# Gate and up products of a SwiGLU layer: one 512-column product for both parts of x, with part of the block sums made earlier

## The chip, the cores and the metric

The kernel runs on one core of a Trainium2 chip (trn2). The metric is the device time of one execution in microseconds. The core has five engines with a queue of instructions each: TensorE (PE in the profile, with its weight loads as PEld), VectorE (DVE), ScalarE (ACT), GpSimd (POOL) and SyncE (SP). An engine takes its instructions in the order in which the program issued them; between engines, semaphores order the work. Here SP only issues DMAs, and POOL mostly does.

## The reference, cut to what matters

An encoder layer on 512 tokens of width 2048: a dilated window attention and a gated linear attention side by side, an output projection, then a SwiGLU feed-forward, all in float32.

```python
h = rmsnorm(x, attn_norm_w[l]);  proj = h @ w_in[l]
...                                    # attention and linear attention
x = x + mixed                          # mixed = concat(...) @ w_out[l]
h = rmsnorm(x, ffn_norm_w[l])          # (512, 2048)
x = x + (jax.nn.silu(h @ w_gate[l]) * (h @ w_up[l])) @ w_down[l]   # FFN_HIDDEN = 5632
return rmsnorm(x, final_norm_w)
```

The change lies in `h @ w_gate` and `h @ w_up`, two products of (512 x 2048) by (2048 x 5632).

## The kernel before

**Precision.** TensorE is given float32 in a rounded form (fp32r). Each operand is split in a rounded part (hi, a cast on ScalarE) and the rounding remainder (lo = value - hi, a subtraction on VectorE), and each product is made three times: hi x hi, hi x lo, lo x hi.

**Gate/up** (class `Feed`, built on `Blocks`). The hidden dimension is cut into 22 stretches of 256 columns; each stretch has a gate unit and an up unit, so there are 44 units, gate and up in turn (the first units are interleaved a little). A unit has 4 pieces of four 128-row blocks of the weight each (512 KB). Weights and tokens are multiplied by a Strassen-Winograd scheme with seven products in place of eight: it needs four sums of weight blocks per piece (`sums`, L1089 to L1091, VectorE), and sums of x made once (`pair_operands`). `split` casts three raw blocks and four summed blocks of a piece (L1101, ScalarE, 768 and 1024 columns), then subtracts (L1106, VectorE). A piece has 2 k-pairs x 7 products x 3 = 42 matmuls of 256 columns (L1147 to L1149); a unit accumulates over its pieces in four PSUM banks (two of the seven results share a bank in three cases). At the end `evac` combines the seven results on VectorE (L1158, L1166) in steps, one step per later piece; a gate unit is multiplied by the token scale (L1184) and goes through Silu (L1185, ScalarE); an up unit is multiplied by that (L1188) and POOL writes the result to `gd` in DRAM (L1190).

**Order.** `run` walks over the pieces. For piece i it issues: loads as slots allow (at most three raw pieces held), the sums of piece i + 2, the split of piece i + 1, the matmuls of piece i, and one step of the `evac` of the unit that ended (`run_urgent`). So the subtraction of piece i + 1 has to be done when TensorE has finished piece i.

**Slots.** SBUF tiles come from two sets, 70 slots of 512 columns (`s2`, a in the profile) and 16 of 1024 (`s4`, b); PSUM is 8 banks (`ps`). A slot that is given back goes to the end of a queue and the one that has been free longest is taken, so with few free ones a slot is soon used again, and its new user waits until the old user's readers are done, a DMA among them.

**Before gate/up.** `jobs` 0 to 5 are the projections for the attention, 6 to 11 those for the linear attention, 12 to 15 (`n_out`) the output projection. `run_job` takes half pieces of weights (512 columns by 128 rows), twelve matmuls of 512 columns each (L285 to L287 and L293 to L295), splits three halves ahead (L196, L197) and, between two halves, lets the attention and linear-attention work (`side`) go on by its rate; so the last attention heads run beside job 6 and the linear attention beside jobs 7 to 12. The down projection follows gate/up; it has its own `Blocks` and isn't touched.

Of the kernel before, what the change touches and what calls it, by code (L numbers as in the profile page):

```python
# [23 lines left out]
P = 128  # L24
# [93 lines left out]
def layer(nc, tc, x, attn_norm_w, w_in, rel_table, gw_f, gb_f, gw_b, gb_b, gla_norm_w, w_out,  # L118
# [7 lines left out]
    with tc.manual_schedule(), \  # L126
# [25 lines left out]
        state = {"credit": 0.0, "set": None}  # L152
# [96 lines left out]
        class Job:  # L249
            drop = None  # L250

# [11 lines left out]
        def run_job(j):  # L263
# [6 lines left out]
            for i in range(j.n):  # L270
# [690 lines left out]
        def half_split(src, n=512):  # L961

            if n == 512:
                hi, lo = s2.get(F32R), s2.get(F32R)
                return (hi, lo), hi.t, lo.t, hi.f
            o = s2.get(F32R, [P, 2, 256])
            return (o,), o.t[:, 0], o.t[:, 1], o.f[:, 0]

        def pair_operands(q, fs_):
# [10 lines left out]
            todo = []  # L980
            slots = []
            for src, n in ((f1.t[:, a], 256), (f2.t, 512), (t13.t, 512), (t24.t, 512)):
                sl, hi, lo, hf = half_split(src, n)
                slots += sl
                todo.append((src, hi, lo, hf))
            for i in range(4):
                src, hi, lo, hf = todo[i]
                act.copy(hi, src)
                sub(lo, src, hf)
                put((f1, f2, t13, t24)[i])  # L990
                if i % 2:
                    yield
            (_, b1h, b1l, _), (_, f2h, f2l, _), (_, t13h, t13l, _), (_, t24h, t24l, _) = todo
            xs[q] = dict(slots=slots, B11=(b1h, b1l), B21=(f2h[:, a], f2l[:, a]), B22=(f2h[:, z], f2l[:, z]),
                         T1=(t13h[:, a], t13l[:, a]), T3=(t13h[:, z], t13l[:, z]),
                         T2=(t24h[:, a], t24l[:, a]), T4=(t24h[:, z], t24l[:, z]))
# [62 lines left out]
        class Blocks:  # L1059
# [9 lines left out]
            def load(self):  # L1069
                while self.n_load < self.n and len(self.raw) < 3 and s4.free:  # L1070
                    w, k, n_kt, col, n = self.source(*self.seq[self.n_load])
                    r = s4.get(F32, self.shape(4))
                    sp.dma_start(out=r.t.rearrange("p a b c -> p (a b c)").rearrange("p (k c) -> p k c", k=n_kt),
                                 in_=w[k * P:(k + n_kt) * P, col:col + n].rearrange("(k p) c -> p k c", p=P))
                    self.raw[self.n_load] = r
                    self.n_load += 1

# [34 lines left out]
        class Feed(Blocks):  # L1112
# [3 lines left out]

            def __init__(self):
# [4 lines left out]
                self.begin(seq, 2, P)  # L1122

# [3 lines left out]

            def products(self, i, banks):
                st_ = self.sets.pop(i)
                piece = self.seq[i][1]  # L1130
                first, last = piece == 0, piece == self.per - 1
                a, z = slice(0, 256), slice(256, 512)
                A, B, C, E = (b.t for b in banks)
                for p in range(2):
                    q = 2 * piece + p
                    (rh, rl), (sh, sl) = st_
                    R = lambda n: (rh.t[:, p, n], rl.t[:, p, n])
                    Z = lambda n: (sh.t[:, p, n], sl.t[:, p, n])
                    x_ = xs[q]
                    prods = [(A[:, a], R(0), x_["B11"], True), (A[:, z], R(2), x_["B21"], False),  # L1140
                             (B[:, a], Z(2), x_["T2"], True), (C[:, a], Z(1), x_["T1"], True),
                             (C[:, z], Z(0), x_["T3"], False), (E[:, a], Z(3), x_["B22"], True),
# [462 lines left out]
```

## Time and profile before

| what | value |
|---|---|
| median of 3 runs | 2231.96 us (2231.88 to 2232.73) |
| the profiled execution's own time | 2234.08 us |
| its span | 2232.3 us |
| granted TensorE clock | 0.999 |
| gate/up stage (first matmul at 869.1, last at 1762.4 us) | 893 us, 7,392 matmuls of 256 columns |
| DMA over the span | 307.78 MB, mean 138 GB/s |

Times in the profile are microseconds. A row of the timeline gives start, duration, engine, line, operation, output <- input, shape and count; what stands in square brackets is how long the engine was idle before it and who released it. Matmuls are pipelined, so a row's duration is longer than the distance to the next one's start; it is the distances that add up. The same holds in part for VectorE and ScalarE, whose operations overlap by up to 0.1 us.

### The profile page before, as it was taken

To read this page: it belongs to the slowest core of one execution; us is meant where nothing else is said; L and a number is where in the kernel's file an instruction comes from. 1 tells how busy PE (TensorE), PEld (TensorE's weight loads), DVE (VectorE), ACT (ScalarE), POOL (GpSimd) and SP (SyncE) were. 2 spreads that over 40 slices of the span, in tenths; PEclk is the share of its full clock that TensorE was granted. 3 is DMA by queue.
4 is the path that set the end of the run, shared out by engine and by line. 5 is a ranking of instruction groups with operands and counts; after the bars stand their busy time and mean duration, and the time that the engine had idled before them with its cause. 6 is when DMAs were issued, how large, how long until landed. Compare 5 with 4: busy or idle time off the path is not lost.

```text
span 2232.3 us, 37013 instructions
## 1 busy us (share of the span) xinstructions
PE 2207.0 (99%) x14814; PEld 2034.4 (91%) x14814; DVE 1635.4 (73%) x2717; ACT 1002.7 (45%) x1637; POOL 116.2 (5%) x173
## 2 busy tenths in 40 slices
PE   8999999999999999999999999999999999999998
PEld 6888888888888888999999999999999999999986
DVE  4366665745454436988888888888888788988877
ACT  5344454444454344444434343444334565555543
POOL 0000000000000100000000000000000110022220
PEclk9999999999999999999999999999999999999999
DMA  6525625232314332333333333333333774588992
GB/s 206 158 68 154 177 79 147 85 123 64 97 57 151 128 127 76 113 115 124 114 114 123 114 123 114 114 125 115 122 120 116 247 179 171 185 198 184 237 372 80
DMA packets 211804, 307.78 MB, mean 138 GB/s; under 512 B 15375, under 2 KB 131263, under 8 KB 211632
## 3 DMA queue, kind: packets, MB, share of 16 engines
q1 hardware_dynamic: 192480, 259.37, 36.1%
q0 software_dynamic: 18256, 44.99, 8.5%
q8 instruction: 116, 1.90, 0.3%
q10 hardware_dynamic: 896, 1.06, 0.1%
q14 instruction: 56, 0.46, 0.1%
HBM read 246.58 MB, written 46.20 MB: 131 GB/s over the span
## 4 chain that ended last, share of the span: by engine, by line
PE 94%; DVE 2%; DMA 2%; ACT 1%; issue 0%; SPq 0%; ACTq 0%; DVEq 0%
PE ps L1149 13%; PE ps L1148 13%; PE ps L1147 13%; PE ps L293 6%; PE ps L294 6%; PE ps L295 6%; PE ps L285 5%; PE ps L287 5%; PE ps L286 5%; PE ps L1376 5%; PE ps L1375 5%; PE ps L1374 5%; PE ps L514 1%; PE ps L841 1%; DMA a<-md 1%; DMA b<-gd 1%
## 5 line engine op out<-in xcount | busy, mean ns | idle before, releaser
L1149 PE MATMUL ps<-a,b 128*128 128x256 f32 x2464 | 697.7, 283 | 2.9 <-DVE b L1106 2.9
L1147 PE MATMUL ps<-a,b 128*128 128x256 f32 x2464 | 697.4, 283 | 0.0
L1148 PE MATMUL ps<-a,b 128*128 128x256 f32 x2464 | 697.3, 283 | 0.0
L1101 ACT CAST b<-b 128x768 fp32r<-128x768 f32 x480 | 445.8, 942 | 533.4 <-DVE b L1106 285.9
L1106 DVE TENSOR_TENSOR b<-b,b 128x768 fp32r<-128x768 f32 x480 | 510.3, 1089 | 132.8 <-PE ps L1148 61.8
L1149 PEld LDWEIGHTS ps<-a,b 128*128 128x128 f32 x2464 | 473.0, 192 | 3.8 <-DVE b L1106 3.8
L1148 PEld LDWEIGHTS ps<-a,b 128*128 128x128 f32 x2464 | 473.0, 192 | 0.0
L1147 PEld LDWEIGHTS ps<-a,b 128*128 128x128 f32 x2464 | 473.0, 192 | 0.0
L197 DVE TENSOR_TENSOR a<-b,a 128x512 fp32r<-128x512 f32 x292 | 195.0, 686 | 126.9 <-ACT a L196 125.7
L1376 PE MATMUL ps<-b,a 128*128 128x256 f32 x896 | 253.7, 283 | 2.7 <-DVE a L1339 2.7
L1375 PE MATMUL ps<-b,a 128*128 128x256 f32 x896 | 253.6, 283 | 0.0
L1374 PE MATMUL ps<-b,a 128*128 128x256 f32 x896 | 253.6, 283 | 0.0
L196 ACT CAST a<-b 128x512 fp32r<-128x512 f32 x292 | 171.1, 617 | 55.8 <-DMA b<-in_w_down_dram 20.9
L293 PE MATMUL ps<-a,a 128*128 128x512 f32 x464 | 183.5, 396 | 0.0
L294 PE MATMUL ps<-a,a 128*128 128x512 f32 x464 | 181.2, 391 | 2.3 <-DVE a L197 2.1
L295 PE MATMUL ps<-a,a 128*128 128x512 f32 x464 | 180.9, 390 | 0.0
L1376 PEld LDWEIGHTS ps<-b,a 128*128 128x128 f32 x896 | 172.0, 192 | 2.9 <-DVE a L1339 2.9
L1375 PEld LDWEIGHTS ps<-b,a 128*128 128x128 f32 x896 | 172.0, 192 | 0.0
L1374 PEld LDWEIGHTS ps<-b,a 128*128 128x128 f32 x896 | 172.0, 192 | 0.0
L1089 DVE TENSOR_TENSOR b<-b 128x512 f32<-128x512 f32 x240 | 164.2, 684 | 7.2 <-DMA b<-in_w_up_dram 4.3
L285 PE MATMUL ps<-a,a 128*128 128x512 f32 x416 | 168.1, 404 | 0.0
L286 PE MATMUL ps<-a,a 128*128 128x512 f32 x416 | 163.1, 392 | 0.0
(224 smaller groups left out, 3071.2 us busy)
## 6 DMA issues: line engine op xcount, KB each, us to landing
b<-in_w_gate_dram SPq DMA_DIRECT2D x88, 512.0 KB, 3.4
b<-in_w_up_dram SPq DMA_DIRECT2D x88, 512.0 KB, 3.4
b<-in_w_down_dram SPq DMA_DIRECT2D x88, 512.0 KB, 5.5
b<-in_w_in_dram SPq DMA_DIRECT2D x96, 256.0 KB, 4.5
b<-in_w_in_dram SPq DMA_DIRECT2D x48, 512.0 KB, 3.8
b<-in_w_out_dram SPq DMA_DIRECT2D x32, 512.0 KB, 4.4
md<-a POOLq DMA_DIRECT2D x56, 256.0 KB, 8.6
a<-a SPq DMA_DIRECT2D x96, 128.0 KB, 2.3
```

The lines of the kernel that those rows point to most:

```text
L285: mm(o, wh.t[:, c], xh.t, start=first, stop=False)
L293: mm(o, xh.t[:, c], wh.t[:, w], start=first, stop=False)
L294: mm(o, xh.t[:, c], wl.t[:, w], start=False, stop=False)
L295: mm(o, xl.t[:, c], wh.t[:, w], start=False, stop=last)
L1101: act.copy(hi.t, src)
L1106: dve.tensor_tensor(lo.t, src, hi.f, op=OP.subtract)
L1147: mm(o, wh, xh, start=head, stop=False, skip_group_check=True)
L1148: mm(o, wh, xl, start=False, stop=False, skip_group_check=True)
L1149: mm(o, wl, xh, start=False, stop=end, skip_group_check=True)
L1374: mm(o, xh[:, t], wh, start=first and h == 0, stop=False, skip_group_check=True)
L1375: mm(o, xh[:, t], wl, start=False, stop=False, skip_group_check=True)
L1376: mm(o, xl[:, t], wh, start=False, stop=last, skip_group_check=True)
```

## The change

In gate/up the tokens' hi and lo parts now lie side by side in one tile of 512 columns, so that hi(weights) x [hi(x), lo(x)] is one matmul of 512 columns instead of two of 256; lo(weights) x hi(x) stays one of 256. The 512 columns fill a bank, so each of the seven results has its own bank, and its two halves have to be added afterwards. Units 0 and 1 keep three matmuls and four banks. The matmuls of a piece are now ordered by result (three that need raw blocks, then four that need summed blocks), and the raw blocks' tiles are given back after the third.

At the end of a unit, `leave` copies all banks to SBUF on ScalarE, seven copies of 512 columns, right after the unit's last matmuls are issued; `evac` then works from SBUF. Its `fold` adds the two halves of a result. In a gate unit results four and five go to one slot of 1024 columns (`two`), so that they are folded by one operation of 512 columns. The instruction order of the changed kernel shows that this slot is in every gate unit the one that the up unit's result (`c_`) has given back one piece earlier, when its write to `gd` had been issued; the fifth copy carries a wait on that DMA.

For 66 of the 176 pieces (every third piece of a unit, and the first of an up unit) the sums are made ahead, in place, by `ff.ahead()`: load on SP, four additions of 256 columns on VectorE, write to DRAM (`sd`) on POOL. `run_job` advances it by 2.4 steps per half piece in jobs 6 to 11 and 1.0 in jobs 12 to 14; a step is one addition. In gate/up such a piece loads its raw blocks and its sums, and `sums` does nothing. `pair_operands` splits x in seven tiles of 256 columns rather than one of 256 and three of 512. `half_split`, now used only by the down projection, moves there unchanged.

```diff
@@ run_job
                     run_side(n)
+                state["ahead"] += j.ahead
+                while state["ahead"] >= 1:
+                    state["ahead"] -= 1
+                    next(state["sums"], None)
             j.evac(banks)
@@ pair_operands
+            for n, (name, f, h) in enumerate((("B11", f1, a), ("B21", f2, a), ("B22", f2, z), ("T1", t13, a),
+                                              ("T3", t13, z), ("T2", t24, a), ("T4", t24, z))):
+                o = xs[q][name] = s2.get(F32R, [P, 2, 256])
+                act.copy(o.t[:, 0], f.t[:, h])
+                sub(o.t[:, 1], f.t[:, h], o.f[:, 0])
...
@@ class Feed(Blocks)
+            PRODUCTS = (("R", 0, "B11"), ("R", 2, "B21"), ("R", 1, "T4"), ("Z", 2, "T2"), ("Z", 1, "T1"),
+                        ("Z", 0, "T3"), ("Z", 3, "B22"))
...
+                self.pre = {i: n for n, i in enumerate(i for i, (u, q) in enumerate(seq) if q == 2 or q == 0 and u % 2)}
+                self.sd = dr.tile([len(self.pre), P, 1024], F32, name="sd")
+            def ahead(self):
...
+                    if todo and len(held) < 2 and len(s4.free) > 1:
+                        r = s4.get(F32, self.shape(4))
+                        self.fetch(todo[0], r)
...
+                    for o, x_ in ((1, 0), (0, 2), (2, 1), (3, 2)):
+                        dve.tensor_tensor(b(o), b(o), b(x_), op=OP.add)
+                        yield
+                    pool.dma_start(out=self.sd[self.pre[i]], in_=r.t.rearrange("p a b c -> p (a b c)"))
+                    put(r)
+            def load(self):
...
+                    if i in self.pre:
+                        S = self.S[i] = s4.get(F32, self.shape(4))
+                        sp.dma_start(out=S.t.rearrange("p a b c -> p (a b c)"), in_=self.sd[self.pre[i]])
...
             def products(self, i, banks):
...
+                        if u > 1:
+                            o = banks[n].t
+                            mm(o, wh, x_.rearrange("p s t -> p (s t)"), start=head, stop=False, **kw)
+                            mm(o[:, 0:256], wl, xh, start=False, stop=end, **kw)
...
+                    if n == 2:
+                        put(rh, rl)
+                put(sh, sl)
+            def leave(self, u, banks):
+                two = s4.get(F32, [P, 2, 512]) if 1 < u < len(self.units) - 2 and u % 2 == 0 else None
...
+                    act.copy(o[:, c], b.t[:, c])
+                    put(b)
...
-            def evac(self, u, banks):
+            def evac(self, u, es, used, two):
...
+                    fold = lambda *ns: [add(es[n][:, a], es[n][:, a], es[n][:, z]) for n in ns]
+                fold(0, 1, 3)
+                add(c[:, a], m2, m1)
+                dve.tensor_tensor(m1, m1, m3, op=OP.subtract)
+                yield
+                if two:
+                    add(m45, m45, two.t[:, :, z])
+                else:
+                    fold(4, 5)
+                if m45 is not None:
+                    add(halves(c[:, 256:768]), m45, m1[:, None, :].to_broadcast([P, 2, 256]))
+                else:
+                    add(c[:, 256:512], m4, m1)
+                    add(c[:, 512:768], m5, m1)
+                add(c[:, 768:1024], m4, c[:, 512:768])
+                yield
+                fold(2, 6)
+                add(c[:, 256:512], c[:, 256:512], m6)
+                add(c[:, 512:768], c[:, 512:768], m7)
+                put(*used, *([two] if two else []))
...
             def run(self):
...
-                        banks[u] = [ps.get() for _ in range(4)]
+                        banks[u] = [ps.get() for _ in range(7 if u > 1 else 4)]
...
-                        urgent.append(self.evac(u, banks.pop(u)))
+                        urgent.append(self.evac(u, *self.leave(u, banks.pop(u))))
@@ layer
+        state["sums"] = ff.ahead()
+        for n, j in enumerate(jobs):
+            j.ahead = 2.4 if 6 <= n < 12 else 1.0 if 12 <= n < n_out else 0.0
```

More of the change, by code (lines that the diff above doesn't have):

```diff
@@ L250, in layer @@
             drop = None
+            ahead = 0.0
         def job(kind, pieces, kts, acts, evac, rate=0.0, before=None, start=None, limit=None):
@@ L1134, in products @@
[L1134 to L1142, printed above, removed]
-                             (E[:, z], R(1), x_["T4"], False)]
-                    for o, (wh, wl), (xh, xl), head in prods:
-                        head = head and first and p == 0
-                        end = last and p == 1
-                        mm(o, wh, xh, start=head, stop=False, skip_group_check=True)
-                        mm(o, wh, xl, start=False, stop=False, skip_group_check=True)
-                        mm(o, wl, xh, start=False, stop=end, skip_group_check=True)
@@ L1574, in layer @@
             if n == n_out:
+                assert next(state["sums"], None) is None
                 ff.run()
```

133 lines of the change are left out of this document (81 added, 52 removed).

## The prediction

> **What bounds the kernel now.** I read the page first, then the busy time by stretches, then single rows of each engine in the gate/up stage.
>
> ```profile
> span 2232.3 us, 37013 instructions
> PE 2207.0 (99%) x14814; PEld 2034.4 (91%) x14814; DVE 1635.4 (73%) x2717; ACT 1002.7 (45%) x1637; POOL 116.2 (5%) x173
> PE 94%; DVE 2%; DMA 2%; ACT 1%; issue 0%; SPq 0%; ACTq 0%; DVEq 0%
> ```
>
> TensorE is 94% of the chain that ended last, so fewer nanoseconds on TensorE shorten the run as long as nothing else takes its place. What could take its place shows only by stage:
>
> ```profile
> core 0: us, PE busy (x) PEld busy (x) DVE busy (x) ACT busy (x) POOL busy (x), PEclk, DMA share, GB/s
> 490.00:720.00 230.00, 229.93 (x1077) 191.87 (x1076) 115.65 (x203) 103.70 (x221) 7.46 (x14) 1.00 0.27 87
> 1380.00:1480.00 100.00, 100.00 (x835) 100.00 (x835) 87.19 (x132) 40.79 (x48) 1.07 (x2) 1.00 0.37 117
> ```
>
> In the gate/up stage (the second row) VectorE is busy for 87 of every 100 us, against 50% beside the linear attention. The stage repeats in pairs of units, one gate and one up, eight pieces, one write of gd per pair:
>
> ```profile
> 1333.26 0.53 POOL L1190 DMA_DIRECT2D gd<-b  x1 [39.78 <-DVE b L1188]
> 1373.59 0.53 POOL L1190 DMA_DIRECT2D gd<-b  x1 [39.80 <-DVE b L1188]
> 745.66 0.39 PE L295 MATMUL ps<-a,a 128*128 128x512 f32 x1
> ...
> 783.74 0.39 PE L295 MATMUL ps<-a,a 128*128 128x512 f32 x1
> ```
>
> A pair takes 40.33 us for its 336 products of 256 columns, 0.1200 us each. In an out-projection stretch without other products, 168 products of 512 columns lie between the last two rows: 38.08 / 168 = 0.2267 us each. A product thus costs its columns and a fixed 13 ns.
>
> **TensorE, removed and added.** Units 0 and 1 keep three products of 256. In the other 42 units (56 groups each, 2,352 in all) three of 256 become one of 512 and one of 256: 0.3600 us becomes 0.3467. That saves 0.0133 x 2352 = 31.4 us and puts TensorE's floor per pair at 112 x 0.3467 = 38.83 us, 1.49 under today's.
>
> The Trainium skill's "TensorE: Matmul & The Clock Gate" (section "Wait — 56ns, not 53.3ns?") has a fixed cost of about 2.5 ns per product; by it the saving would be 6 us. The rows above measure 13 ns, and the measurement decides. With the bound found below, the forecast is the same by either.
>
> **VectorE and ScalarE per pair.** Prices are distances from one start to the next:
>
> ```profile
> 1346.58 0.69 DVE L1158 TENSOR_TENSOR a<-ps,a 128x512 f32<-128x512 f32 x1
> ...
> 1348.24 0.68 DVE L1089 TENSOR_TENSOR b<-b 128x512 f32<-128x512 f32 x1
> 1348.96 0.42 DVE L1090 TENSOR_TENSOR b<-b,b 128x256 f32<-128x256 f32 x1
> 1349.42 0.42 DVE L1091 TENSOR_TENSOR b<-b,b 128x256 f32<-128x256 f32 x1
> 1349.76 2.09 DVE L1106 TENSOR_TENSOR b<-b,b 128x768 fp32r<-128x768 f32 x2
> 1351.76 1.29 DVE L1184 TENSOR_TENSOR b<-b,a 128x512 f32<-128x512 f32 x2
> 1352.97 0.69 DVE L1089 TENSOR_TENSOR b<-b 128x512 f32<-128x512 f32 x1
> ...
> 1361.70 0.42 DVE L1158 TENSOR_TENSOR b<-ps,a 128x256 f32<-128x256 f32 x1
> 1362.04 0.41 DVE L1166 TENSOR_TENSOR a<-a,ps 128x256 f32<-128x256 f32 x1
> 1362.37 0.68 DVE L1089 TENSOR_TENSOR b<-b 128x512 f32<-128x512 f32 x1
> ...
> 1372.07 1.22 DVE L1188 TENSOR_TENSOR b<-b,b 128x1024 f32<-128x1024 f32 x1
> 1373.21 0.68 DVE L1089 TENSOR_TENSOR b<-b 128x512 f32<-128x512 f32 x1
> ```
>
> A piece's sums (L1089 to L1091) take 1.52 us and its split (L1106, twice) 2.01. An operation of 256 columns takes 0.33, or 0.46 when the next needs its result; one of 512 takes 0.60 or 0.72; the up multiply 1.14 and 1.22 to its end. Removed per pair: three of eight sums, 4.56 us, and the old combination (2 x 0.67 + 2 x 1.66 = 4.7, from the rows 1361.70 and 1346.58 to the next sums). Added: folds and sums in three steps. Step 1 is five operations of 256 (1.67); step 2 two of 512 in a chain and one of 256 for gate (1.78), five of 256 for up (1.80); step 3 four of 256 (1.46) before the old multiply. VectorE's work per pair goes from about 35.2 to 36.0 us. That alone fits under 38.83; the question is whether VectorE must also wait.
>
> It must, at two places, since each unit now ends with seven 512-column copies on ScalarE (leave), and these stand in ScalarE's queue ahead of the next piece's casts, for which VectorE's next subtraction waits.
>
> ```profile
> 1353.14 1.06 ACT L1185 ACTIVATE b<-b 128x1024 f32<-128x1024 f32 x1 [5.39 <-DVE b L1184]
> 1354.11 2.68 ACT L1101 CAST b<-b 128x768 fp32r<-128x768 f32 x3
> ...
> 1372.19 0.84 ACT L1101 CAST b<-b 128x768 fp32r<-128x768 f32 x1 [1.43 <-DVE b L1106]
> 1374.74 1.05 ACT L1101 CAST b<-b 128x1024 fp32r<-128x1024 f32 x1 [1.72 <-PE ps L1148]
> 1376.85 1.79 ACT L1101 CAST b<-b 128x768 fp32r<-128x768 f32 x2 [1.05 <-DMA gd<-b]
> 1954.08 1.07 ACT L1393 COPY a<-ps 128x512 f32<-128x512 f32 x2
> 1955.03 0.44 ACT L1335 ACTIVATE a<-b 128x256 fp32r<-128x256 f32 x1
> ```
>
> (a) During an up unit: the Silu of the gate before it (0.09 after the multiply, which ends at 1353.05, and 0.97 to the next start) is queued ahead of the up unit's copies (7 x 0.475 from the last two rows = 3.33), then the cast of three blocks (0.84). From the gate multiply's end to the next subtraction: 5.23 us. VectorE has one sum and one split in between, 3.5 us.
>
> (b) At the end of a gate unit: two copies go to a 1024-column slot, and the order of allocations shows that it is always the slot that the up result has just left, so copy five waits until the gd write has landed. By the rows, the multiply ends at 1373.29 and the cast that waits for gd starts at 1376.85: 3.56 us. Then three copies (1.43) and the cast (0.84): 5.83 us.
>
> Around the loop, all on VectorE, ScalarE and this write: split 2.10 (its second cast, 1.05 us, ends 0.09 after the first subtraction), step 1 1.67, sums 1.52, split 2.01, step 2 1.78, sums 1.52, split 2.01, step 3 with the multiply to its end 2.75 (15.36 in all); chain (a) 5.23; the same for up without the second sums and with 1.80 and 2.81 for its steps 2 and 3, 13.92; chain (b) 5.83. Together 40.34 us per pair, over TensorE's 38.83 and beside today's 40.33. TensorE then waits some 1.5 us per pair, first for the rounding remainders of a gate unit's first piece. The 31 us go into a new wait.
>
> ```profile
> gd<-b POOLq DMA_DIRECT2D x22, 512.0 KB, 3.2
> b<-in_w_gate_dram SPq DMA_DIRECT2D x88, 512.0 KB, 3.4
> b<-in_w_out_dram SPq DMA_DIRECT2D x32, 512.0 KB, 4.4
> ```
>
> The gd write's time is the least certain term. A pair moves twelve transfers of 512 KB where it moved nine (three reads of sd), 117 GB/s becoming about 157. Transfers of this size land after 3.4 us in this stage and 4.4 in the out-projection, so the write gains between 0 and 1.0 us; I take 0.3, nearer to gd's own row. The loop is 40.64, or +0.31 x 21 pairs = +7 us (0 to +21).
>
> The seven banks cost nothing: the next unit wants the bank of copy n one group after copy n's own group came round, a piece (4.9 us) later, and chain (b) holds copy five for about 2.4; without that cover each late bank would stop TensorE itself.
>
> **The sums made ahead** are 264 additions of 256 columns, 66 loads on SP between those of w_in, and 66 writes on POOL (0.53 each to issue, ahead of the residual loads on that queue). About 56 fall beside the last attention heads:
>
> ```profile
> 302.53 0.68 DVE L197 TENSOR_TENSOR a<-b,a 128x512 fp32r<-128x512 f32 x1
> 303.99 0.69 DVE L566 CUSTOM_DVE_ANT_0 a<-ps,b 128x512 f32<-128x512 f32 x1 [0.77 <-PE ps L554]
> 306.36 0.69 DVE L197 TENSOR_TENSOR a<-b,a 128x512 fp32r<-128x512 f32 x1
> 307.66 0.69 DVE L566 CUSTOM_DVE_ANT_0 a<-ps,b 128x512 f32<-128x512 f32 x1 [0.61 <-PE ps L554]
> ```
>
> VectorE idles 0.77 and 0.61 us per step there and gets 2.2 additions, some 0.8 us: just full, and I cost it at 2 us (0 to 10, were each of 26 steps 0.4 late). Beside the linear attention 160 additions (59 us) lie in 114 us of idle time; a load that lands late blocks what is queued behind the addition on VectorE, the splits first, which run three half pieces ahead. I cost that at 1 us. If the cover were gone, the work would cost 264 x 0.37 = 98 us. Rounding x in pieces of 256 adds well under 1 us before the first gate product. The reads of sd are issued at least a piece ahead, 4.9 us against 3.4, and cost nothing while that holds; each one late costs its lateness.
>
> **Sum.** The profiled execution took 2234.08 us around its span of 2232.3, 2.1 above the median of the runs: 2234.1 + 7 + 3 + 0.5 = 2244.6, as a median 2242.5; I say 2242.
>
> **Rivals.** *TensorE stays the bound.* If the loop is 1.8 us shorter than I make it, all 31.4 us stay: 2232 - 31.4 + 3.5 = 2204. For it: VectorE's 36.0 us do fit, the groups that need remainders of the sums come 2 us into a piece, and partial relief gives a time in between. Against: both chains are in-order queues with measured lengths. *The gd write lands later still.* From 3.86 us on each further microsecond adds 21; at 1.2 more it is 2267. For it: the raw and sd loads for the next unit are released just before it. Against: the write's own row is 3.2. *The front becomes VectorE's.* If the additions hold up the attention and linear-attention steps by 0.4 us in 60 of them, 24 us are added where the sum has 3: about 2263; against it the 50% of 490 to 720.
>
> **How the numbers follow.** Forecast 0.46 (own range 2228 to 2254), TensorE still the bound or nearly so 0.25 (2201 to 2226), late gd write 0.17 (2254 to 2275), front 0.12 (2250 to 2268). About 0.2% (4.5 us) can be told from no change. Faster: 0.25 + 0.03 of the forecast's lower edge = 0.28; same: 0.17 of the forecast and 0.02 of the front = 0.19; slower: the rest, 0.53. The range runs from TensorE's floor, 2202, to 2258; it leaves out most of the late-write and half of the front's case.
>
> **What would show it.** Right: a gd-to-gd distance of 40.4 to 41 us; TensorE idle for 1 to 2 us per pair, put down to VectorE's split; ScalarE's fifth copy waiting for gd; VectorE waiting 1.5 to 2.5 us for ScalarE's cast once per unit. Wrong: a distance of 38.8 to 39.5 with TensorE unbroken (the chains overlap where I lined them up), copies spaced other than 0.48, or TensorE gaps before 880 us.

## The result and the profile after

| | before | after |
|---|---|---|
| median, same chip | 2232.35 us (2231.88 to 2235.78) | 2313.38 us (2310.93 to 2317.37) |
| ratio | | 1.0357 (95%: 1.0344 to 1.0369) |
| span of the profiled execution | 2232.3 us | 2315.6 us |

The change makes the kernel 3.6% slower. The forecast was 2242 us, with a range up to 2258; the direction was right, the size was not: 81 us instead of 10.

The page of the changed kernel: span, busy time by engine, and the shares of the chain that ended last.

```profile
span 2315.6 us, 33557 instructions
PE 2230.8 (96%) x12462; PEld 1915.5 (83%) x12462; DVE 1741.5 (75%) x3147; ACT 1133.6 (49%) x1919; POOL 151.3 (7%) x239
issue 49%; PE 40%; DMA 4%; DVE 3%; POOL 2%; ACT 1%; SPq 0%; POOLq 0%; ACTq 0%; DVEq 0%
```

TensorE was 94% of the chain of the kernel before and is 40% now. The 49% of "issue" is time for which the page has no name, so the chain is of no use here, and the stages have to be read. The writes of gd cut the run in three: the first and the last of 22, of the kernel before and of the changed one.

```profile
930.06 0.54 POOL L1190 DMA_DIRECT2D gd<-b  x1 [59.20 <-DVE b L1188]
...
1771.49 0.53 POOL L1190 DMA_DIRECT2D gd<-b  x1 [34.50 <-DVE b L1188]
```

```profile
953.58 0.54 POOL L1262 DMA_DIRECT2D gd<-b  x1 [59.96 <-DVE b L1260]
...
1854.88 0.53 POOL L1262 DMA_DIRECT2D gd<-b  x1 [41.58 <-DVE b L1260]
```

Up to the first write 23.5 us are lost. The 21 distances between the writes took 841.4 us and take 901.3, 59.9 more (42.92 us a pair on average). What follows the last write takes 460.8 and 460.7. Together 83.3, the difference of the two spans. So there are two losses: the loop over the pairs, and the front, where the sums are made ahead.

**The loop.** Windows, waits and transfers of the changed kernel (an engine's wait: total us, times, longest):

```profile
1380.00:1480.00 100.00, 95.35 (x523) 79.78 (x523) 81.64 (x134) 51.69 (x73) 1.60 (x3) 1.00 0.46 154
```

```profile
ACT b L1210 <- DMA gd<-b: 84.5, 20, 7.2
PEld ps L1187 <- DVE b L1098: 60.1, 77, 1.4
...
PEld ps L1186 <- ACT b L1210: 6.9, 12, 3.1
```

```profile
b<-in_w_gate_dram SPq DMA_DIRECT2D x110, 512.0 KB, 4.1
gd<-b POOLq DMA_DIRECT2D x22, 512.0 KB, 5.4
```

VectorE is busy for less of the stage than before (82 of 100 us against 87), and still TensorE stands: all engines wait for each other. The one wait that every pair has (20 times, 4.2 us each) is that of a leave copy for the gd write, which lands 5.4 us after its issue; it was 3.2. One such place in the timeline:

```profile
1469.07 1.22 DVE L1260 TENSOR_TENSOR b<-b,b 128x1024 f32<-128x1024 f32 x1
...
1470.32 0.37 SPq L1067 DMA_DIRECT2D b<-in_w_up_dram  x1
1470.59 0.53 POOL L1262 DMA_DIRECT2D gd<-b  x1 [42.24 <-DVE b L1260]
...
1475.94 1.07 ACT L1210 COPY b<-ps 128x512 f32<-128x512 f32 x2 [4.17 <-DMA gd<-b]
...
1478.27 2.17 DVE L1098 TENSOR_TENSOR b<-b,b 128x768 fp32r<-128x768 f32 x2 [4.45 <-ACT b L1093]
```

```profile
1499.00 2.17 DVE L1098 TENSOR_TENSOR b<-b,b 128x768 fp32r<-128x768 f32 x2 [1.73 <-ACT b L1093]
```

The up multiply ends at 1470.29. It frees two things at once: the gd write on POOL, and the slot of the gate, which the next raw load on SP takes. SP is 0.27 us quicker. From the multiply's end to copy five are 5.65 us, where the prediction had 3.86. VectorE's two waits for a cast are 4.45 us (the prediction's chain b) and 1.73 us (its chain a).

**The front.** The stretch beside the last attention heads, of the kernel before and of the changed one:

```profile
400.00:460.00 60.00, 59.93 (x316) 50.44 (x314) 41.54 (x92) 29.98 (x65) 0.00 (x0) 1.00 0.35 107
```

```profile
400.00:460.00 60.00, 49.26 (x234) 39.89 (x233) 41.98 (x100) 22.59 (x48) 3.19 (x6) 0.91 0.54 182
...
420.00:430.00 10.00, 4.62 (x17) 4.13 (x18) 4.97 (x10) 2.18 (x5) 0.26 (x1) 0.69 0.45 153
...
425.38 0.80 PE L558 MATMUL ps<-a,a 128*128 128x512 f32 x1 [6.09 <-DVE a L668]
```

TensorE gets through 234 products instead of 316. VectorE is no busier than before (42.0 us of 60 against 41.5), and the granted clock of TensorE falls to 0.69 in one stretch where it mostly stands. The Trainium skill's "TensorE: Matmul & The Clock Gate" (section "What's actually happening") has the clock fall after an idle window of some 3.4 us; the trace agrees in so far as the clock in the second row is low where TensorE stood for 5.4 of 10 us, and the last row has it standing for 6.09 us in one go. What VectorE and SP waited for between 340 and 480 us:

```profile
DVE b L1146 <- DMA b<-in_w_up_dram: 12.8, 6, 6.1
DVE b L1146 <- DMA b<-in_w_gate_dram: 9.3, 6, 4.9
```

```profile
SPq L181 <- DMA sd<-b: 32.8, 6, 8.2
```

VectorE stands for 22.1 us before additions of the sums ahead (L1146) whose raw piece has not landed. SP also holds the projections' own weights (L181) back until a slot comes free from a write to sd; that alone says little, because in the kernel before SP waits 96 us at the same line in the same window, for other users of its slots. How far the work fell back shows between two operations of VectorE that both kernels have:

```profile
374.97 0.68 DVE L649 TENSOR_TENSOR a<-ps,a 32x512 f32<-32x512 f32 x1 [10.28 <-ACT a L648]
...
411.06 1.28 DVE L663 SCALAR_TENSOR_TENSOR a<-ps,a 128x512 f32<-128x512 f32 x2
```

```profile
376.11 0.68 DVE L654 TENSOR_TENSOR a<-ps,a 32x512 f32<-32x512 f32 x1 [3.42 <-ACT a L653]
...
424.29 0.43 DVE L1146 TENSOR_TENSOR b<-b 128x256 f32<-128x256 f32 x1 [4.86 <-DMA b<-in_w_gate_dram]
424.64 1.28 DVE L668 SCALAR_TENSOR_TENSOR a<-ps,a 128x512 f32<-128x512 f32 x2
```

36.1 us became 48.5; over half of the front's loss lies in this one stretch. L668 stands in VectorE's queue right behind an addition that waited 4.86 us for its raw piece, and it is L668 that TensorE waited 6.09 us for.

### The profile page after: what moved, and what is told of

The parts are those of the page before. It is cut to its first block, busy times and chain, and to the rows that moved or that the text cites. A ratio compares the mean times of both kernels' runs of the same rounds, so it can differ in the third digit from the quotient of the medians.

```text
span 2315.6 us, 33557 instructions
## 1 busy us (share of the span) xinstructions
PE 2230.8 (96%) x12462; PEld 1915.5 (83%) x12462; DVE 1741.5 (75%) x3147; ACT 1133.6 (49%) x1919; POOL 151.3 (7%) x239
## 4 chain that ended last, share of the span: by engine, by line
issue 49%; PE 40%; DMA 4%; DVE 3%; POOL 2%; ACT 1%; SPq 0%; POOLq 0%; ACTq 0%; DVEq 0%
PE ps L295 4%; PE ps L296 4%; PE ps L294 4%; PE ps L286 4%; PE ps L288 4%; PE ps L287 4%; PE ps L1457 2%; PE ps L1456 2%; PE ps L1455 2%; POOL md L1477 2%; PE ps L519 1%; DMA b<-in_w_gate_dram 1%; PE ps L846 1%; PE ps L1634 1%; PE ps L1635 1%
## 5 line engine op out<-in xcount | busy, mean ns | idle before, releaser
L1186 PE MATMUL ps<-a,b 128*128 128x512 f32 x2352 | 836.1, 398 | 4.2 <-ACT b L1210 3.5
L1187 PE MATMUL ps<-a,b 128*128 128x256 f32 x2352 | 668.7, 284 | 35.7 <-DVE b L1098 34.5
L1093 ACT CAST b<-b 128x768 fp32r<-128x768 f32 x480 | 430.8, 953 | 365.3 <-DVE b L1098 243.1
L1186 PEld LDWEIGHTS ps<-a,b 128*128 128x128 f32 x2352 | 442.2, 188 | 115.4 <-ACT b L1210 6.9
L1187 PEld LDWEIGHTS ps<-a,b 128*128 128x128 f32 x2352 | 444.8, 189 | 60.1 <-DVE b L1098 60.1
L295 PE MATMUL ps<-a,a 128*128 128x512 f32 x464 | 183.3, 395 | 5.9 <-DVE a L197 5.7
L294 PE MATMUL ps<-a,a 128*128 128x512 f32 x464 | 185.2, 399 | 1.1 <-ACT a L1210 1.1
L296 PE MATMUL ps<-a,a 128*128 128x512 f32 x464 | 182.5, 393 | 0.0
L286 PE MATMUL ps<-a,a 128*128 128x512 f32 x416 | 168.4, 405 | 0.0
L1210 ACT COPY a<-ps 128x512 f32<-128x512 f32 (+1 forms) x262 | 140.8, 600 | 51.6 <-PE ps L1187 36.7
L288 PE MATMUL ps<-a,a 128*128 128x512 f32 x416 | 163.5, 393 | 2.3 <-DVE a L197 2.3
L287 PE MATMUL ps<-a,a 128*128 128x512 f32 x416 | 163.3, 392 | 0.0
L1146 DVE TENSOR_TENSOR b<-b 128x256 f32<-128x256 f32 x264 | 108.7, 421 | 37.9 <-DMA b<-in_w_up_dram 24.6
```

The source lines that it names most:

```text
L286: mm(o, wh.t[:, c], xh.t, start=first, stop=False)
L288: mm(o, wl.t[:, c], xh.t, start=False, stop=last)
L294: mm(o, xh.t[:, c], wh.t[:, w], start=first, stop=False)
L295: mm(o, xh.t[:, c], wl.t[:, w], start=False, stop=False)
L296: mm(o, xl.t[:, c], wh.t[:, w], start=False, stop=last)
L1093: act.copy(hi.t, src)
```

## The experiments

All runs in one table; the ratio is against the kernel before on the same chip, the two columns at the right come from the gd writes as above (first write; mean of the 21 distances). Beside the rows below, the median of the kernel before was 2232.4 to 2235.8 us, so medians of different rows compare to some 3 us.

| run | median us | ratio (95%) | first gd | a pair |
|---|---|---|---|---|
| before | 2232.35 | | 930.1 | 40.07 |
| after | 2313.38 | 1.0357 (1.0344 to 1.0369) | 953.6 | 42.92 |
| no_two | 2292.01 | 1.0255 (1.0238 to 1.0272) | 950.8 | 41.79 |
| three_256 | 2322.80 | 1.0391 (1.0375 to 1.0406) | 955.9 | 43.14 |
| gd_on_sp | 2258.50 | 1.0099 (1.0080 to 1.0117) | 955.0 | 40.27 |
| sp_after | 2257.06 | 1.0102 (1.0085 to 1.0119) | 953.1 | 40.23 |
| sp_behind | 2266.15 | 1.0141 (1.0126 to 1.0156) | 955.3 | 40.57 |
| pool_swap | 2246.78 | 1.0056 (1.0041 to 1.0071) | 951.6 | 39.75 |
| late_sums | 2297.01 | 1.0273 (1.0258 to 1.0289) | 936.0 | 42.90 |
| deep | 2315.64 | 1.0361 (1.0346 to 1.0377) | 954.8 | 42.89 |
| deep2 | 2310.56 | 1.0338 (1.0323 to 1.0353) | 951.9 | 42.89 |
| no_adds | 2290.17 | 1.0259 (1.0243 to 1.0274) | 929.5 | 42.85 |
| adds_free | 2316.75 | 1.0368 (1.0354 to 1.0381) | 955.6 | 42.93 |
| adds_paced | 2311.33 | 1.0345 (1.0328 to 1.0363) | 952.4 | 42.90 |
| sp_no_two | 2228.82 | 0.9971 (0.9962 to 0.9980) | 934.9 | 39.70 |
| sp_17 | 2230.85 | 0.9980 (0.9970 to 0.9989) | 933.3 | 39.71 |
| sp_no_two_256 | 2241.60 | 1.0038 (1.0024 to 1.0052) | 933.0 | 40.44 |
| swap_late | 2224.25 | 0.9956 (0.9941 to 0.9971) | 935.4 | 39.40 |
| swap_late_no_two | 2228.31 | 0.9973 (0.9962 to 0.9983) | 932.4 | 39.76 |

### Is it the loop, and is TensorE out of it?

**no_two** gives the second half of a gate unit no slot of its own.

```diff
-                two = s4.get(F32, [P, 2, 512]) if 1 < u < len(self.units) - 2 and u % 2 == 0 else None
+                two = None
```

> All seven results of every unit are copied to 512-column slots, so no copy waits for the gd write. Theory (the pair of units is paced by a loop VectorE - ScalarE - gd write; the write lands 5.4 us after it is issued and holds copy five for 4.2 us): the wait goes, the fold of results four and five costs VectorE nothing more (1.80 against 1.78 us), the gd-to-gd distance falls from 42.9 to 39.0 to 39.8 us and the time from 2313 to 2230 to 2250. Rival (VectorE's own work and the Silu chain are the bound, the gd wait only fills idle time): 41.5 us or more per pair, 2280 or more.

A miss: 2292, a pair 41.79 us, the rival's numbers. But the wait did not go, it found another victim. The slot that the gd write holds is now taken by the next piece's cast, which waits 20 times, 52.3 us in all (the copies had waited 84.5):

```profile
1459.23 2.70 ACT L1093 CAST b<-b 128x768 fp32r<-128x768 f32 x3 [2.21 <-DMA gd<-b]
```

With slots handed out in the order in which they came back, taking one user away only moves the wait to the next.

**three_256** takes the 512-column product apart again (as two of 256 in the halves of the same bank), and leaves all else as changed.

```diff
-                            mm(o, wh, x_.rearrange("p s t -> p (s t)"), start=head, stop=False, **kw)
+                            mm(o[:, 0:256], wh, xh, start=head, stop=False, **kw)
+                            mm(o[:, 256:512], wh, xl, start=False, stop=False, **kw)
```

> The product of 512 columns is undone, three of 256 columns in the same seven banks; all else as changed. Theory (TensorE is not the bound of gate/up any more): 42.7 to 43.3 us per pair, 2308 to 2322, though TensorE has 31 us more to do. Rival (TensorE's time still counts on top of the waits): 44.4 us per pair, 2344.

2322.8 (0.8 above the theory's range, with its 43.14 us a pair inside), 9.4 us more than with the 512-column product, of the 31.4 that TensorE would need: in the changed kernel most of that saving lies in TensorE's standing.

### Why does the gd write land late?

**gd_on_sp** has SP issue the write, so that it stands in SP's queue ahead of the raw load.

```diff
-                    pool.dma_start(out=gd[j], in_=c)
+                    sp.dma_start(out=gd[j], in_=c)
```

> The gd write is issued by SP instead of POOL, ahead of the raw load that the same up multiply releases. Theory (the write lands late because that raw load is issued 0.3 us before it and shares the engines): the write lands after about 3.4 us, copy five waits 2 us less, 40.7 to 41.3 us per pair, 2271 to 2283. Rival (the reads of sd make every transfer slower): the write still takes 5 us, 42.5 us or more, 2305 or more.

```profile
1438.95 1.23 DVE L1260 TENSOR_TENSOR b<-b,b 128x1024 f32<-128x1024 f32 x1
...
1440.20 0.34 SPq L1262 DMA_DIRECT2D gd<-b  x1
1440.59 0.43 SPq L1067 DMA_DIRECT2D b<-in_w_up_dram  x1
...
1443.26 1.07 ACT L1210 COPY b<-ps 128x512 f32<-128x512 f32 x2 [1.62 <-DMA gd<-b]
```

One line is worth 55 us (2258.5, where 2271 to 2283 were expected): the write lands in 3.0 us, and a pair takes 40.27 us. But the edit changes two things, the queue and the order.

**sp_after** was to keep SP and put the write behind the load (it issues the write at the start of the next piece instead of at once).

```diff
@@ evac, up unit
-                    pool.dma_start(out=gd[j], in_=c)
-                    put(c_)
+                    if u < len(self.units) - 1:
+                        self.later = (j, c, c_)
...
@@ run, next piece
                     self.load()
+                    if self.later:
+                        jj, cc, cs = self.later
+                        sp.dma_start(out=gd[jj], in_=cc)
+                        put(cs)
...
```

> The changed kernel with the gd write issued by SyncE, but just behind the next raw load instead of ahead of it; all else as changed. Theory (the write lands late because the load that was issued ahead of it takes the same engines first): the write lands 5 us or more after its issue, a pair takes 42 to 43 us, 2295 to 2315 us in all. Rival (GpSimd's queue itself makes the write slow): it lands after about 3 us, a pair 40.3 to 41 us, 2258 to 2275 us.

It settled nothing: the raw load that the multiply frees came later in SP's program still, and the write went out ahead of it as in gd_on_sp, with the same time. **sp_behind** puts it right behind that load: `flush` issues the write that is held and gives its slot back.

```diff
...
@@ load, behind the loads of a piece
+                    self.flush()
...
@@ evac, up unit
-                    pool.dma_start(out=gd[j], in_=c)
-                    put(c_)
+                    if u < len(self.units) - 1:
+                        self.later = (j, c, c_)
...
```

> The changed kernel with the gd write issued by SyncE just behind the raw load that the same multiply sets free; sp_after was meant to be this, but there the write still went out ahead of that load. Theory A (what is issued first takes the transfer engines first): the write lands 5 us or more after its issue, a pair takes 42 us or more, 2295 to 2315 us in all. Theory B (the order does not matter much, a write from GpSimd's queue is late whenever a load of SyncE is in flight): it lands in 3 to 3.8 us, a pair 40.3 to 40.8 us, 2258 to 2270 us.

```profile
1443.18 0.37 SPq L1074 DMA_DIRECT2D b<-in_w_up_dram  x1
1443.60 0.50 SPq L1068 DMA_DIRECT2D gd<-b  x1
```

```profile
gd<-b SPq DMA_DIRECT2D x22, 512.0 KB, 5.1
```

Theory A is right on the landing: 5.1 us from SP's own queue, 0.4 us behind one load of the same size, against 3.0 ahead of it. It is wrong on the time: 2266 and not 2295 or more, and a pair of 40.57 us, which are theory B's numbers, because the slot is also given back a step later here, and ScalarE waited for the write only 15 us in the whole run. Lateness costs nothing by itself, but only through whoever takes the slot next.

**pool_swap** leaves the write on POOL and swaps two names: the written slot is given back ahead of the gate's.

```diff
-                    put(self.gate)
                     pool.dma_start(out=gd[j], in_=c)
-                    put(c_)
+                    put(c_, self.gate)
```

> The changed kernel, the gd write on GpSimd's queue as before, but the two slots given back in the other order: the next raw load then takes the slot that the write reads and waits for its landing, and the leave copies take the gate's slot. Both theories of the late write: no load is in flight beside the write, so it lands in about 3.2 us and no copy waits for it; a pair 39.7 to 40.6 us, 2245 to 2265 us in all. Rival (the load that now starts 3 us later is late for its own sums and casts): a pair 41.5 us or more, 2283 us or more.

```profile
1430.50 0.53 POOL L1261 DMA_DIRECT2D gd<-b  x1 [39.06 <-DVE b L1260]
...
1432.24 1.29 ACT L1210 COPY b<-ps 128x512 f32<-128x512 f32 x2
1433.42 0.37 SPq L1067 DMA_DIRECT2D b<-in_w_up_dram  x1
```

As both theories had it: the load now waits for the write (2.9 us after its issue, POOL's queue is no slower than SP's), the copies take the gate's slot and wait for nothing, and a pair takes 39.75 us. So it is the load ahead of it that makes the write late. The Trainium skill's "DMA: Bandwidth & Descriptors" (section "Queues, rings and completion order") has each transfer engine work through one queue in its order and take turns between queues, packet by packet; the landing times fit both rules, though no row here shows the packets: 5.1 us behind a load in one queue, 5.4 beside it in two, 2.9 to 3.0 with nothing issued just ahead.

### What does the front lose?

**late_sums** spreads the same 264 additions over jobs 8 to 14, past the attention heads.

```diff
-            j.ahead = 2.4 if 6 <= n < 12 else 1.0 if 12 <= n < n_out else 0.0
+            j.ahead = 3.0 if 8 <= n < 12 else 2.0 if 12 <= n < n_out else 0.0
```

> The sums made ahead begin two jobs later, after the attention heads (3.0 steps in jobs 8 to 11, 2.0 in 12 to 14); the same 264 additions, loads and writes. Theory (the first gate product is 23 us late because VectorE, already full beside the attention heads, waits there for the loads): 18 to 22 us come back, 2291 to 2295, gate/up unchanged at 42.9 us per pair. Rival (the additions and their transfers cost this time wherever they lie): 2308 or more.

16.4 us came back in the medians (19 by the two ratios), the first gd write at 936.0, 17.6 earlier: the theory's lower edge, and far from the rival; the pairs are unchanged. The front and the loop are separate accounts. VectorE still stands for 20.3 us before additions whose raw piece has not landed (34.6 in the whole run of the changed kernel), but all of it after 500 us, beside the linear attention, and the first gd write comes only 5.9 us later than in the kernel before. So it counts not only how long VectorE stands, but what stands behind it.

**deep** was to hold up to four raw pieces (`len(held) < 2` to `< 4`).

> The changed kernel with raw pieces for the sums ahead fetched up to four in advance instead of two or fewer; all else as changed. Theory (the front lost its 23.5 us by VectorE waiting for raw pieces that land 5 us after their issue): the first gd write comes 10 us or more sooner than 953.6 us, 2295 to 2304 us in all. Rival (VectorE's own work on the sums is the cost, the waits only show where it stands): the first gd write within 4 us of 953.6, 2309 to 2317 us.

It says nothing: `load` is called once for each piece, so never more than two are held and no instruction changed. It is a second measurement of the changed kernel (2315.6). **deep2** really loads a piece earlier, for the first 25 pieces or so.

```diff
-                    if todo and len(held) < 2 and len(s4.free) > 1:
+                    while todo and len(held) < (3 if len(todo) > 40 else 2) and len(s4.free) > 1:
```

> The changed kernel with the raw pieces for about the first 25 sums ahead held up to three at a time, so that each is loaded a piece earlier; the additions keep their places. Theory (standing still for raw pieces): the first gd write comes 8 us or more before 953.6, 2296 to 2306 us in all. Rival (the additions' own time, or the slots that the earlier loads take from the attention): within 4 us of 953.6, or later, 2309 us or more.

A miss for the theory, 1.7 us earlier instead of 8: the earlier loads need slots earlier, and SP then waits longer at L181 for the writes to sd that hold them (49.1 us between 300 and 480 us, 32.8 in the changed kernel).

**no_adds** leaves the additions out and keeps loads and writes.

```diff
-                        dve.tensor_tensor(b(o), b(o), b(x_), op=OP.add)
```

> The changed kernel without the 264 additions of the sums ahead: raw pieces are loaded, held and written out as before, but not summed, so the second operands of 66 pieces are raw blocks and the output is another. Theory (the front's loss is VectorE's: its additions and its standing still before them for raw pieces, with the attention's own operations behind): the first gd write comes at 930 to 937 us, 2290 to 2297 us in all. Rival (the loss is slots and transfers: the attention's weights wait for slots that the sd writes hold): it stays at 945 us or later, 2304 us or more.

The first gd write comes at 929.5: all of the front's loss is gone, although the transfers are all there. So the loss needs an addition in VectorE's queue. Is it the addition's 0.4 us, or the standing before it? **adds_free** adds from one piece that is already there, so that no addition waits.

```diff
...
-                        dve.tensor_tensor(b(o), b(o), b(x_), op=OP.add)
+                        dve.tensor_tensor(z.t[:, :, o], r.t[:, :, o], r.t[:, :, x_], op=OP.add)
...
```

> The changed kernel with its 264 additions ahead in their places, but from one raw piece that lies in its slot from the start, into another slot: 65 of the 66 loads are left out, no addition waits for a transfer, the 66 writes to sd stay and carry that one piece, so the output is another. Theory (the front's loss is VectorE standing still before additions whose raw piece has not landed, with the attention's operations behind): the first gd write comes at 930 to 938 us, 2290 to 2298 us in all. Rival (the additions' own 0.4 us each in a stretch where VectorE has no room): 945 us or later, 2304 us or more.

By its first gd write and its time it misses (955.6, 2316.75: the rival's numbers), but for a reason of its own: nothing paced the writes any more, 22 of the 66 were issued between 356 and 396 us, the transfer engines were busy throughout (first row, 367 GB/s), and VectorE waited 26.88 us for ScalarE, which waited for a transfer between two SBUF tiles. From there on the additions stand without waits, and the stretch to the last row takes 39.75 us:

```profile
356.00:396.00 40.00, 23.19 (x102) 16.83 (x100) 10.02 (x22) 3.51 (x7) 11.64 (x22) 0.83 1.01 367
...
395.50 0.68 DVE L654 TENSOR_TENSOR a<-ps,a 32x512 f32<-32x512 f32 x1 [26.88 <-ACT a L653]
...
435.25 1.28 DVE L668 SCALAR_TENSOR_TENSOR a<-ps,a 128x512 f32<-128x512 f32 x2
```

**adds_paced** is adds_free, but adds into a fresh slot each time and writes that one, so that the writes keep their pace.

```diff
+                    z = s4.get(F32, self.shape(4))
...
-                    pool.dma_start(out=self.sd[self.pre[i]], in_=r.t.rearrange("p a b c -> p (a b c)"))
+                    pool.dma_start(out=self.sd[self.pre[i]], in_=z.t.rearrange("p a b c -> p (a b c)"))
+                    put(z)
```

> adds_free with each write tied to its additions again: the additions read one raw piece that lies in its slot and write a fresh slot, and that slot is written to sd after the fourth addition; 65 loads are left out, so the output is another. Theory (VectorE stands still for raw pieces; the additions' own time is little): the stretch from L654's first row to L668's, 48.5 us in the changed kernel and 36.1 in the one before, takes 39 to 41 us (39.75 in adds_free), the first gd write comes at 934 to 942 us, 2293 to 2302 us in all. Rival (the additions' own time and the slots that the writes hold): 44 us or more, first gd at 946 us or later, 2305 us or more.

The rival's numbers came: first gd 952.4, and the stretch 50.25 us:

```profile
374.72 0.68 DVE L654 TENSOR_TENSOR a<-ps,a 32x512 f32<-32x512 f32 x1 [8.95 <-ACT a L653]
...
424.63 0.43 DVE L1134 TENSOR_TENSOR b<-b 128x256 f32<-128x256 f32 x1 [4.29 <-DMA sd<-b]
424.97 1.28 DVE L668 SCALAR_TENSOR_TENSOR a<-ps,a 128x512 f32<-128x512 f32 x2
```

VectorE's waits before additions within this stretch, of adds_paced and of the changed kernel:

```profile
DVE b L1134 <- DMA sd<-b: 11.2, 4, 4.3
```

```profile
DVE b L1146 <- DMA b<-in_w_gate_dram: 6.5, 3, 4.9
...
DVE b L1146 <- DMA b<-in_w_up_dram: 1.7, 2, 1.2
```

In adds_paced the addition needs no load, but its fresh slot is one that a write to sd still holds, and VectorE stands for that. So the theory as I had written it (waiting for raw pieces) is too narrow. Put together as a sum, for the stretch that takes 36.1 us in the kernel before: additions without such waits cost 3.7 us more (adds_free, 39.75); 3.7 and the changed kernel's 8.2 us of waits make 11.9, where 12.4 were lost; 3.7 and the 11.2 us of adds_paced make 14.9, where 14.2 were lost; 3.7 and the 9.0 us of deep2 make 12.7, where 14.3 were lost (its stretch takes 50.37); without additions it is 0.8 (no_adds, 36.88). What fits these runs, to 1.6 us, is VectorE standing before an addition whose 512 KB are late, be it the piece or the slot, with the attention queued behind; the additions' own time is then the smaller part. The 3.7 us are the weak term: in adds_free the stretch follows a long stop and has no writes to sd beside it. No run takes the waits away and leaves all else; what they would be with slots to spare was not tried.

### What is the rest of the change worth?

**sp_no_two** joins gd_on_sp, no_two and late_sums. **sp_17** is the same with `two` kept, a slot of 1024 columns more and two of 512 fewer.

```diff
-N2 = 70
-N4 = 16
+N2 = 68
+N4 = 17
```

> The changed kernel with three edits together: the gd write issued by SyncE ahead of the next raw load, no rounded slot of its own for the second half's low part (as in the kernel before), and the sums ahead spread over more of the attention with none at its end. Theory (the loop's two chains and the late write were the whole loss; the sums ahead the rest): with the write out of the way the leave copies wait for the write no more than 1.6 us, a pair takes 38.9 to 39.5 us, so the loop is at TensorE's floor of 38.83 us, and the first gd write comes at 935 to 940 us: 2205 to 2225 us in all, likeliest 2213, ahead of the kernel before. Rival (the copies and the two roundings bound it however the write goes): a pair stays at 40.2 us or more, 2238 us or more.

> The changed kernel with the gd write on SyncE, the sums ahead spread as in sp_no_two, the second half's slot kept, and one more rounded slot of four (17 for 16, two slots of two fewer). Theory: with a slot more, the slot that the gd write frees is taken one step later, so no leave copy waits for it; a pair 38.9 to 39.5 us, 2210 to 2222 us in all. Rival (the wait is for VectorE's subtraction, not for slots): a pair 40.0 us or more, 2235 us or more.

In both loops TensorE waits for less than 1 us in all, as the theory had it, at 39.7 us a pair: a little over its 38.9 to 39.5 and under the rivals' 40.2 and 40.0. The times are 4 and 9 us above the theory's ranges; most pairs run at 39.57 us and not at 38.83 (below). The two versions are 0.3% and 0.2% ahead of the kernel before.

**sp_no_two_256** is sp_no_two with the product taken apart as in three_256.

> sp_no_two with the one 512-column product taken apart into two of 256 columns again, in halves of the same bank: what the product is worth where TensorE is busy all the time. Theory (the prediction's 0.0133 us of each of 2352 groups, 31 us): 2256 to 2262 us in all, a pair 40.9 to 41.2 us. Rival (sp_no_two's pair of about 39.3 us with a full TensorE says 0.3510 us a group and not 0.3467, so 0.0090 us a group, 21 us): 2247 to 2252 us, a pair 40.3 us.

Below both in time: 2241.6, a pair 40.44 us on average and 40.32 in the steady ones (the rival's pair), just the kernel before's pace. With TensorE the bound the product is worth 0.75 us a pair there (40.32 - 39.57), some 13 us in the medians and 15 by the two ratios, neither 31 nor 21.

**swap_late** joins pool_swap and late_sums; **swap_late_no_two** adds no_two.

> pool_swap with the sums ahead spread as in late_sums: two cures, each by itself worth 66.6 and 16.4 us on the changed kernel. Theory (they lie one after the other and add): the first gd write at 934 to 937 us, a pair 39.7 us, 2227 to 2233 us in all, level with the kernel before or just ahead. Rival (with TensorE full in the loop the front's gain is lost again): 2236 us or more.

> swap_late without the slot of its own for two results of a gate unit. Theory (TensorE is already the bound there, at 39.3 to 39.7 us a pair): within 3 us of swap_late. Rival (chain (b) still holds it for part of each pair): 4 to 8 us faster than swap_late.

swap_late has the lowest median, 3 us below the expected 2227 to 2233 and 0.44% ahead of the kernel before (0.29 to 0.59), by two small edits. Without `two` the median is 4 us higher, against both expectations; but the intervals overlap, and swap_late's own runs go from 2220.8 to 2232.5 us, so the two are not told apart. In the profiled run swap_late's first half goes at 39.57 us a pair and its second at 38.83. TensorE is fully busy in both; the change comes at a short stop (the middle row; 569 products in the 100 us up to 1317 us, 578 in the 100 us from 1320):

```profile
1000.00:1100.00 100.00, 100.00 (x568) 86.77 (x567) 90.83 (x151) 58.30 (x82) 1.59 (x3) 1.00 0.48 158
...
1318.67 0.39 PE L1187 MATMUL ps<-a,b 128*128 128x256 f32 x1 [0.61 <-DVE b L1098]
...
1600.00:1700.00 100.00, 100.00 (x579) 88.22 (x577) 93.32 (x157) 58.30 (x80) 1.59 (x3) 1.00 0.50 167
```

## Why the prediction was right or wrong

**TensorE's saving: right in kind, and only partly within reach.** The floor of 38.83 us a pair is what swap_late shows in the second half of its profiled run. The sp versions run mostly at 39.57, and there the product is worth half as much (0.75 us a pair, not 1.49). In the changed kernel itself most of it lies in waits, as predicted.

**The loop of VectorE, ScalarE and the gd write: right.** VectorE stands at the two places named. Chain (a) was to leave it 5.23 - 3.5 = 1.73 us idle, and the row says 1.73. The sum of 40.34 us a pair, with 3.56 for the write, would be 39.86 with gd_on_sp's 3.08 (1440.18 to 1443.26) and 42.43 with the changed kernel's 5.65; measured are 40.27 and 42.92. So it is 0.4 to 0.5 us short in both, and otherwise holds. A small slip on the way: the prediction's terms for VectorE's work add up to 35.8 us a pair, not 36.0; swap_late shows 35.9 (90.83 of 100 us, at 39.57 a pair), and nothing hung on it.

**The gd write's lateness: the term that failed.** The prediction took 0.3 us more than in the kernel before, from the landing times of loads in two stages, with an upper bound of 1.0; it was 2.1 (5.65 where 3.56 stood). The rows that it used are medians over all transfers of a kind; what counted is which transfer stands just ahead of this one: behind one raw load the write lands after 5.1 to 5.4 us, without it after 2.9 to 3.0. The rival "the gd write lands later still" named that reason, "the raw and sd loads for the next unit are released just before it", and got 0.17. By its own rule (21 us for each further microsecond) 2.1 us is 38 us more than the forecast.

**The front: also mis-sized, 3 us taken, 23.5 measured.** VectorE's room beside the attention heads was worked out (0.8 us of additions against gaps of 0.6 to 0.8), the wait of an addition for its load was seen only beside the linear attention, and it was costed at 1 us. It struck beside the heads, where VectorE's queue has the attention behind it: the rival "the front becomes VectorE's" had the 24 us, by another mechanism (0.4 us of work in 60 steps). What the runs showed in its place: without additions the loss is gone (no_adds), with the same additions moved past the heads three quarters of it are gone (late_sums), and in the stretch that lost 12.4 us VectorE stood 8.2 us before additions whose raw piece was late.

**The two rivals did not exclude each other.** Both happened, and the range was drawn as if only one could. Forecast 10.5 us; the loop's missing 42.92 - 40.64 = 2.28 us a pair, 48 us (the late write's 38, and 10 by which the sum is short); the front's missing 20 us; and 5.3 us because the last pair in the kernel before took 35.0 us and not 40.3 as the product with 21 had it: together 84, and the spans differ by 83.3.

**What was said to cost nothing.** The sums ahead cost the loop nothing in their reads: with the two waits cured (swap_late) TensorE waits 0.6 us in the whole loop. The seven banks cost something, but little: weight loads waited 6.9 us in all for the leave copies.

## What to carry to other kernels

When one instruction frees two things at once, look at which transfer goes out first: a write that somebody waits for belongs ahead of a prefetch that nobody needs yet, and the order in which slots are given back decides who waits for it. Before work is put into an idle engine's gaps, ask not only whether the gaps hold it but what stands behind it in the queue when its data are late. And where two rivals can happen together, the range has to hold their sum.

## What the runs showed of the hardware that was not expected

- A 512 KB write to DRAM lands 2.9 to 3.2 us after its issue with no transfer issued just ahead (pool_swap 2.9, gd_on_sp 3.0, the kernel before 3.2), and 5.1 to 5.6 us behind one load of the same size issued 0.3 to 0.4 us earlier, from either queue (sp_behind 5.1 from SP; the changed kernel 5.4 and no_two 5.6 from GpSimd).
- TensorE has two paces for the same instructions with no wait, full busy time and a granted clock of 1.00: 39.57 and 38.83 us for 112 groups of a 512- and a 256-column product (0.3533 and 0.3467 us a group). swap_late went from one to the other after the stop of 0.61 us at 1318 us. swap_late_no_two had a like stop there and stayed at the slower pace throughout; sp_no_two and sp_17 left the slower one only for a few pairs (576 products in 1400 to 1500 us of sp_17, 568 in the 100 us after). What decides it was not tried; three products of 256 ran at 40.32 throughout.
